# Half of an output projection inside the attention, operand pieces in a pool of nine, and four column blocks ahead of the last norm

## The chip, the cores and the metric

The kernel runs on one core of a Trainium2 chip. The metric is the device time of one execution in microseconds (us), the median of several runs. The core has five engines with queues of their own: TensorE (PE) for matrix products and transposes, VectorE (DVE), ScalarE (ACT), GpSimd (POOL), and SyncE (SP), which here issues nearly all DMA transfers. Each engine works through its own list in order; between engines the work is ordered by semaphores.

## The reference, cut

One layer of an encoder over two groups of tokens, a prompt of 512 and a sample of 1024, in float32. Attention and a state-space scan work side by side on each group; their outputs are gated, added and projected, then a norm, a residual sum and a SwiGLU feed-forward follow.

```python
proj = h @ w_in
att = rmsnorm(diff_attention(q, k, v, lam, rel_bias), subln_w) * (1.0 - lam_init)
y_ssm = rmsnorm((y_f + y_b + d_skip * xs) * silu(z), ssm_norm_w)
merged = g[:, :, 0] * (att @ w_proj_attn) + g[:, :, 1] * (y_ssm @ w_proj_ssm)
x = x + rmsnorm(merged @ w_out, norm_post_mix)
h = rmsnorm(x, norm_pre_ffn)
gate, up = split(h @ w_gate_up)
x = x + rmsnorm((silu(gate) * up) @ w_down, norm_post_ffn)
```

The model width is 1024 (8 blocks of 128), the feed-forward 2816 wide (22 blocks of 128).

## The kernel before

All products are made from split operands: a float32 value is a high part (`hi`) and the rest (`lo`), and each product of two 128-row blocks takes three matmuls (`gemm`, lines 167 to 169). `split` makes the two parts; "act_dve" casts on ACT (L135) and subtracts on DVE (L136), "act_pool" casts on ACT (L141) and subtracts on POOL (L142). `split_panel` does so for a 1024 x 256 weight panel. The code issues work in program order, and a scheduler that runs a timeline model while the kernel is built then settles each engine's order; pools of tiles with a fixed number of buffers set when a tile can be reused.

The stages: input projections; prompt attention and scans; then the three that matter here.

- `ph2`: the sample's attention, 8 heads of 8 query tiles of 128. A query tile needs scores on PE, a bias and minimum (L296) on DVE, an exponential (L299) on ACT, an addition of the two softmax maps (L304, `last_add`), transposes (L308), copies and lower parts (L311, L312), and the product with v into `o`. The attention gives way (`yield`) 64 times in all, and each time `run` adds `RATIO` to what is due of `side_work`, which has 32 units: the prompt's `w_proj_attn` (into `m_d`) and `w_proj_ssm` of three chunks of 512 tokens (`part_d`). After the last head, `mean_square` (L326, L327) sums squares of the output.
- `ph3`, first part. `load_merged(0)` reads the prompt's merged rows back and splits them (L891, L892). `att_scale(1)` makes the scales of the sample's heads (L334 to L344) and stores them in `r_d`. `aT1 = att(1)` loads, for each of eight heads, the attention rows and the scales (L349, L351), multiplies them (L352) and splits them, in a ring `araw` of three buffers. Then `out_proj(m0)`, `merge(1, aT1)`, `norms(0)`, `att(2)`, `out_proj(m1)`, `merge(2)`, `norms(1)`, `out_proj(m2)`, `norms(2)`. `out_proj` is 384 matmuls of 256 columns with copies and sums of squares on ACT (L1048, L1050); `norms` (L1057 to L1080) applies the post-norm, adds the input rows (L1065 to L1067), stores `x2_d`, applies the pre-norm (L1074), transposes on PE (L1078) and stores `h2_d`.
- The feed-forward. `Operands` reads `h2_d` for 768 tokens and makes seven operands `b11, t2, t3, t1, b21, t4, b22` (a seven-product scheme for two-by-two blocks); `t4` is three subtractions and additions on data of `b21` and `t2` (L951 to L953). `weights(jb)` makes the seven weight combinations of a column block, four of them on POOL (L989 to L997). `gate_up` does seven products of 12 matmuls with 384 columns, 84 a block. Blocks `jb < NPRE` come before `norms(2)`; after all 22, a second set of operands is made for the other 768 tokens, with `t4` and `b22` on POOL, and 22 more blocks follow. A last stage is the down projection.

The pool `big` holds seven tiles of 16 KB a partition: first the split pairs of `m` and `aT`, later one tile for each operand.

Of the kernel before, what the change touches and what calls it, by code (L numbers as in the profile page):

```python
# [18 lines left out]
P = 128  # L19
D = 1024  # L20
# [13 lines left out]
OT = ("gt", 2)  # L34
NG = 2
YE = ("act_pool",) * 4
RATIO = 0.5
QS = 0
IA = 1
AHEAD = (0,)  # L40
XRB = 2
NPRE = 2
CB = (1, 1)
RWB = 7
NW = 0
NKEEP = 1
SEQS = ((0, 4), (4, 12))
GROUPS = ((0, 512), (512, 1024))
# [29 lines left out]
def hybrid_trunk_kernel(ctx: ExitStack, tc: tile.TileContext, a: dict, y_prompt, y_sample):  # L78
# [5 lines left out]
    def f(ap):  # L84
        return ap.bitcast(F32)
# [26 lines left out]
    r_d = [dram.tile([32 * n, P], F32, name=f"r_d{n}") for n in (1, 2)]  # L112
    m_d = dram.tile([D, 512], F32, name="m_d")
    part_d = dram.tile([D, T], F32, name="part_d")
    x2_d = dram.tile([T, D], F32, name="x2_d")
    h2_d = dram.tile([D, T], F32, name="h2_d")
    ff_d = [dram.tile([DFF, 768], F32, name=f"ff_d{g}") for g in range(2)]
# [679 lines left out]

    ap = ctx.enter_context(tc.tile_pool(name="ap", bufs=1, reuse_waits="tile"))
    zq, msq = [ap.tile([P, 8, 8], F32, name=n) for n in ("zq", "msq")]
    with ExitStack() as ph2:  # L800
        qr = ph2.enter_context(tc.tile_pool(name="qr", bufs=2, reuse_waits="tile"))
        qk = ph2.enter_context(tc.tile_pool(name="qk", bufs=2, reuse_waits="tile"))
# [34 lines left out]
        def side_work():  # L837
            ahead = y_rows(0)
            aTt = yt.tile([P, 2, KB, 512], F32R, tag="yT", name="aTt", bufs=1)
            load_att(0, (aTt[:, 0], aTt[:, 1]), lambda: [t_[:, i] for t_ in [rp.tile([P, 2, 512], F32, tag="wraw", name="wraw")]  # L840
                                                 for i in range(2)])
            for r0 in range(0, D, P):
                gt = gated(r0, 0, slice(0, 512), panel(a["w_proj_attn"][0][:, r0:r0 + P]), (aTt[:, 0], aTt[:, 1]))
                store(out=m_d[r0:r0 + P, :], in_=gt)
                yield

            for c in range(NCH):
                cs = slice(c * 512, (c + 1) * 512)
                yTt = yt.tile([P, 2, KB, 512], F32R, tag="yT", name="yTt", bufs=1)
                for i_, raw in enumerate(ahead):  # L850
                    for j in (0, 2):
                        k = i_ * 4 + j
                        split(yTt[:, 0, k:k + 2], yTt[:, 1, k:k + 2], raw[:, j:j + 2], YE[k // 2])
                ahead = y_rows(c + 1)
                for r0 in range(0, D, P):
                    gt = gated(r0, D, cs, panel(a["w_proj_ssm"][0][:, r0:r0 + P]), (yTt[:, 0], yTt[:, 1]))
                    if c == 0:
                        mt = rp.tile([P, 512], F32, tag="wraw", name="mt")
                        load(out=mt, in_=m_d[r0:r0 + P, :])
                        G.tensor_add(gt, gt, mt)  # L860
                    store(out=part_d[r0:r0 + P, cs], in_=gt)
                    yield

        side = side_work()
        run(heads(512, 1024, range(8), pend, zq, msq, qk, pp, at, qr, s_ps, t_ps, o_ps),
            side, RATIO)
        for _ in side:
            pass
        pend.pop()()


    with ExitStack() as ph3:
        big = ph3.enter_context(tc.tile_pool(name="big", bufs=7, reuse_waits="tile"))
        wk = ph3.enter_context(tc.tile_pool(name="wk", bufs=2, reuse_waits="tile"))
        wy = ph3.enter_context(tc.tile_pool(name="wy", bufs=1, reuse_waits="tile"))
        mm = ph3.enter_context(tc.tile_pool(name="mm", bufs=6, space=PSUM, reuse_waits="tile"))
# [3 lines left out]
        def mm_tile(n):  # L880
            return mm.tile([P, n], F32, tag="mm", name="mm")

        def big_pair():
            return [big.tile([P, KB, 512], F32R, tag="big", name="big") for _ in range(2)]

        def load_merged(c):
            hi, lo = big_pair()
            for k in range(0, KB, 2):
                both = mp.tile([P, 2, 512], F32, tag="mt", name="both", bufs=4)
                load(out=both, in_=part_d[k * P:(k + 2) * P, c * 512:(c + 1) * 512].rearrange("(a p) t -> p a t", p=P))  # L890
                S.activation(out=hi[:, k:k + 2], in_=both, func=AF.Copy, scale=0.5)  # L891
                V.scalar_tensor_tensor(lo[:, k:k + 2], both, 0.5, f(hi[:, k:k + 2]), op0=ALU.mult, op1=ALU.subtract)  # L892
            return hi, lo

        def merge(c, aTt):
            cs = slice(c * 512, (c + 1) * 512)
# [20 lines left out]
        class Operands:  # L917
# [4 lines left out]
            def __init__(self, t0, pool, tag, bufs):  # L922
                self.t0, self.pool, self.tag, self.bufs, self.tiles = t0, pool, tag, bufs, {}
# [4 lines left out]
                load(out=x, in_=h2_d[r0:r0 + P, n0:n0 + 384])  # L928
                return x

            def build_first(self):
                b11, t2, t3, t1 = [big.tile([P, 2, 4, 384], F32R, tag="big", name="op") for _ in range(4)]
                self.tiles.update(b11=b11, t2=t2, t3=t3, t1=t1)
                for k in range(4):
                    x, y, z = self.raw(0, 0, k), self.raw(0, 1, k), self.raw(1, 1, k)
                    split(b11[:, 0, k], b11[:, 1, k], x[:], "act_dve")
                    V.tensor_sub(z, z, y)
                    split(t3[:, 0, k], t3[:, 1, k], z[:], "act_dve")
                    V.tensor_sub(y, y, x)
                    split(t1[:, 0, k], t1[:, 1, k], y[:], "act_dve")  # L940
                    V.tensor_add(x, x, z)
                    split(t2[:, 0, k], t2[:, 1, k], x[:], "act_dve")

            def build(self, names, add, eng):
                for name in names:
# [89 lines left out]
        with ExitStack() as ph3a:  # L1035
# [48 lines left out]
                return load_att(c, big_pair(), lambda: [  # L1084
                    wk.tile([P, 512], F32, tag="araw", name="araw", bufs=3) for _ in range(2)])

            m0 = load_merged(0)
            att_scale(1, zq, msq, ap, tr_ps, "tr")
            aT1 = att(1)
            t0 = out_proj(m0)  # L1090
            m1 = merge(1, aT1)
            norms(0, t0)
            aT2 = att(2)
# [2 lines left out]
            norms(1, t1)  # L1096
            ops = Operands(0, wk, "araw", 3)
            ops.build_first()
            ops.build(("b21",), V, "act_dve")
            t2 = out_proj(m2)  # L1100
            ops.build(("t4",), V, "act_dve")
            ops.tag, ops.bufs = OT
            ops.build(("b22",), V, "act_pool")
            w = {jb: weights(jb, "pt", 1) for jb in range(NPRE + NW)}
            for jb in range(NPRE):
                gate_up(0, jb, ops.all(), w[jb], mp, 1, False)
            norms(2, t2)

        with tc.tile_pool(name="fw", bufs=2, reuse_waits="tile") as fw:
            for jb in range(NPRE, FB):  # L1110
                if jb >= NPRE + NW:
                    w[jb] = weights(jb, rpool=fw if jb > NPRE else None)
# [99 lines left out]
```

## Time and profile before

| | |
|---|---|
| median of 3 runs | 3193.3 us (3192.85 to 3196.85) |
| the profiled execution | 3197.76 us |
| its span in the profile | 3196.0 us |
| mean granted clock of PE | 0.978 of full speed |
| PE busy over the span | 3044.8 us |
| DVE, ACT, POOL busy | 1837.5, 1256.7, 681.7 us |

A row of the profile names the line, the engine, the operation, and output and inputs by the program's names, with the time it was busy; "idle before" is the time in which that engine waited, and the arrow names the instruction that ended the wait. PEclk is the clock granted to PE, 1.00 being full speed.

### The profile page before, as it was taken

The page shows a single profiled execution, that of the slowest core. Times are in us where ns is not written, and L with a number is a line of the kernel's source. Part 1 is how long each engine was busy: PE and PEld are TensorE (multiplying, and loading weights), DVE is VectorE, ACT ScalarE, POOL GpSimd, SP SyncE. Part 2 cuts the span into 40 slices and gives each one's busy share as a digit, 9 for nine tenths or more (in the row PEclk, how much of TensorE's full clock was granted, in tenths as well). Part 3 has the DMA queues.
Part 4 walks back from the last instruction along what each step waited for, and adds up shares of the span by engine and source line. Part 5 has one row for each costly group of instructions (what it writes and reads, how often), then busy time and mean ns, then how long its engine had stood idle before and what let it go on. Part 6 is the DMA issues. An engine that isn't in the chain of part 4 may idle for free. (4 is left out here: it accounts for less than half of the span.)

```text
span 3196.0 us, 44151 instructions
## 1 busy us (share of the span) xinstructions
PE 3044.8 (95%) x16667; PEld 2677.0 (84%) x16667; DVE 1837.5 (57%) x2953; ACT 1256.7 (39%) x2301; POOL 681.7 (21%) x520
## 2 busy tenths in 40 slices
PE   8999999999999999899999898978999899989998
PEld 7988887888887777788888787878999899978787
DVE  5214444455327996387878955686667765632444
ACT  4103333333303333366666645543333333332343
POOL 0001111000133442243332100023333433210100
PEclk9999999999999999999999999989999999999999
DMA  4633333123554444755546047644333333363454
GB/s 149 195 99 113 112 104 106 57 79 106 152 170 136 147 143 149 212 173 167 165 137 186 27 139 239 218 141 136 103 98 105 97 103 91 114 203 97 124 163 132
DMA packets 443165, 430.35 MB, mean 135 GB/s; under 512 B 25232, under 2 KB 360305, under 8 KB 441841
## 3 DMA queue, kind: packets, MB, share of 16 engines
q1 hardware_dynamic: 442953, 427.55, 43.3%
q8 instruction: 131, 2.15, 0.3%
q14 instruction: 81, 0.66, 0.1%
HBM read 315.40 MB, written 120.44 MB: 136 GB/s over the span
## 5 line engine op out<-in xcount | busy, mean ns | idle before, releaser
L167 PE MATMUL acc<-hT,whi 128*128 128x512 f32 x1056 | 421.4, 399 | 4.0 <-ACT st L453 4.0
L168 PE MATMUL acc<-hT,whi 128*128 128x512 f32 x1056 | 416.7, 395 | 0.0
L169 PE MATMUL acc<-hT,wlo 128*128 128x512 f32 x672 | 262.2, 390 | 0.0
L167 PEld LDWEIGHTS acc<-hT,whi 128*128 128x128 f32 x1056 | 199.0, 188 | 50.2 <-issue 5.8
L299 ACT ACTIVATE pt<-pt,nm 128x1024 f32<-128x1024 f32 (+1 forms) x192 | 193.1, 1006 | 109.9 <-DVE nm L296 106.6
L168 PEld LDWEIGHTS acc<-hT,whi 128*128 128x128 f32 x1056 | 199.1, 189 | 42.7 <-issue 3.6
L296 DVE CUSTOM_DVE_ANT_0 pt<-s,tb 128x1024 f32<-128x1024 f32 (+1 forms) x192 | 197.5, 1041 | 52.4 <-PE s L294 40.4
L167 PE MATMUL acc<-whi,hT 128*128 128x256 f32 x768 | 225.2, 293 | 1.2 <-DVE st L374 0.6
L169 PE MATMUL acc<-whi,hT 128*128 128x256 f32 x768 | 225.6, 294 | 0.5 <-DVE hT L207 0.3
L168 PE MATMUL acc<-wlo,hT 128*128 128x256 f32 x768 | 224.2, 292 | 0.0
L169 PE MATMUL d<-dhi,fl 128*128 128x512 f32 x528 | 207.8, 393 | 8.9 <-DVE fl L136 8.9
L167 PE MATMUL d<-dhi,fh 128*128 128x512 f32 x528 | 207.7, 393 | 6.8 <-ACT fh L135 6.8
L168 PE MATMUL d<-dlo,fh 128*128 128x512 f32 x528 | 207.1, 392 | 0.0
L135 ACT CAST whi<-wraw 128x1024 fp32r<-128x1024 f32 (+1 forms) x115 | 115.9, 1036 | 213.8 <-PE acc L169 83.1
L136 DVE TENSOR_TENSOR fl<-raw,fh 128x896 fp32r<-128x896 f32 (+1 forms) x72 | 86.0, 1195 | 198.1 <-ACT fh L135 190.2
L234 POOL TENSOR_TENSOR ql<-raw,qh 128x512 fp32r<-128x512 f32 x48 | 65.3, 1373 | 577.3 <-ACT qh L231 567.9
L167 PE MATMUL mm<-op,wy 128*128 128x384 f32 x528 | 178.8, 339 | 9.5 <-ACT op L135 7.3
L169 PE MATMUL mm<-op,wy 128*128 128x384 f32 x528 | 178.6, 338 | 0.0
L168 PE MATMUL mm<-op,wy 128*128 128x384 f32 x528 | 178.3, 338 | 0.0
L136 DVE TENSOR_TENSOR wlo<-wraw,whi 128x1024 fp32r<-128x1024 f32 x80 | 97.1, 1243 | 114.9 <-ACT whi L135 105.6
L135 ACT CAST fh<-raw 128x896 fp32r<-128x896 f32 (+1 forms) x72 | 70.8, 983 | 225.8 <-PE d L168 189.9
L167 PEld LDWEIGHTS acc<-whi,hT 128*128 128x128 f32 x768 | 148.3, 193 | 12.1 <-issue 10.0
(358 smaller groups left out, 8325.0 us busy)
## 6 DMA issues: line engine op xcount, KB each, us to landing
wraw<-in_w_in_dram SPq DMA_DIRECT2D x60, 512.0 KB
wraw<-in_w_gate_up_dram SPq DMA_DIRECT2D x92, 256.0 KB
raw<-ff_d SPq DMA_DIRECT2D x48, 448.0 KB
wr<-in_w_gate_up_dram SPq DMA_DIRECT2D x80, 256.0 KB
ff_d<-c SPq DMA_DIRECT2D x88, 192.0 KB
g_d<-st SPq DMA_DIRECT2D x48, 256.0 KB
xg<-xs_d SPq DMA_DIRECT2D x48, 256.0 KB
gt<-g_d SPq DMA_DIRECT2D x48, 256.0 KB
```

The costliest lines, as they stand in the source:

```text
L135: S.copy(hi, raw)
L136: V.tensor_sub(lo, raw, f(hi))
L167: TE.matmul(ps, ah, bh, start=(i == 0), stop=False)
L168: TE.matmul(ps, ah, bl, start=False, stop=False)
L169: TE.matmul(ps, al, bh, start=False, stop=(i == n - 1))
L234: G.tensor_sub(q_l[:, s_], q_r[:, s_], f(q_h[:, s_]))
L296: V.tensor_tensor_reduce(out=pt[:], in0=sps[:], in1=tb[:, off:off + SL], scale=-1.0, scalar=3.0e38, op0=ALU.add, op1=ALU.min, accum_out=nm ...
L299: S.activation(out=pt, in_=pt, func=AF.Exp, bias=nm[:, m:m + 1], scale=-1.0, accum_out=(z0, zs[:, 0:1])[m])
```

## The change

It does four things.

1. The pool `big` becomes nine tiles of 12 KB. A pair of `m` or `aT` takes three tiles (class `Part` finds the part and block); an operand takes one.
2. `out_proj(m0)` goes from `ph3` into `side_work` as 16 units of 24 matmuls, with `RATIO` at 0.625, so 40 units are taken during the heads. The first eight use the buffer `f_ps`; the last eight (`LATE`) use score buffers `s_ps` and are tied behind the last addition by `issue_after`. Results go to `mo_d`, the sums of squares to `sums0`, and `ph3` loads them back as `t0`. `pend.pop` and `att_scale(1)` are issued ahead of the last eight units.
3. `t4` is issued together with `b21`, ahead of `out_proj(m2)`; the first weights are issued ahead of `b22`, whose splits now use DVE for the lower part. `NPRE` is 4, and weights are issued block by block.
4. In the second operand set `b11` and `t2` are issued first, with `t2`'s additions on POOL, then `t3` and `t1`, with DVE.

```diff
-RATIO = 0.5
+RATIO = 0.625
+LATE = 8
-NPRE = 2
+NPRE = 4
-NW = 0
...
+            m0 = yt.tile([P, 2, KB, 512], F32R, tag="yT", name="m0", bufs=1)
+            for k in range(0, KB, 2):
+                both = rp.tile([P, 2, 512], F32, tag="wraw", name="both")
+                load(out=both, in_=part_d[k * P:(k + 2) * P, 0:512].rearrange("(a p) t -> p a t", p=P))
+                S.activation(out=m0[:, 0, k:k + 2], in_=both, func=AF.Copy, scale=0.5)
+                V.scalar_tensor_tensor(m0[:, 1, k:k + 2], both, 0.5, f(m0[:, 0, k:k + 2]), op0=ALU.mult, op1=ALU.subtract)
+            for i in range(16):
+                p0, j = i // 4 * 256, i % 4
+                if j == 0:
+                    w = split_panel(a["w_out"][0][:, p0:p0 + 256])
+                if i < 16 - LATE:
+                    ps = f_ps.tile([P, 512], F32, tag="f", name="f")[:, 0:256]
+                else:
+                    ps = s_ps.tile([P, 1024], F32, tag="s", name="late")[:, 0:256]
+                with tc.issue_after(last_add[-1].ins) if i >= 16 - LATE else nullcontext():
+                    gemm_tm(ps, w, (m0[:, 0], m0[:, 1]), slice(j * P, (j + 1) * P))
+                mo = yt.tile([P, 512], F32, tag="gt", name="mo")
+                S.copy(mo[:, 0:256], ps)
+                S.activation(out=mo[:, 256:512], in_=ps, func=AF.Square, accum_out=sums0[:, j, i // 4:i // 4 + 1])
+                store(out=mo_d[j * P:(j + 1) * P, p0:p0 + 256], in_=mo[:, 0:256])
+                yield
...
+        pend.pop()()
+        att_scale(1, zq, msq, ap, t_ps, "t")
         for _ in side:
             pass
-        pend.pop()()
...
-        big = ph3.enter_context(tc.tile_pool(name="big", bufs=7, reuse_waits="tile"))
+        big = ph3.enter_context(tc.tile_pool(name="big", bufs=9, reuse_waits="tile"))
...
         def big_pair():
-            return [big.tile([P, KB, 512], F32R, tag="big", name="big") for _ in range(2)]
+            tiles = [big.tile([P, 2, 3, 512], F32R, tag="big", name="big") for _ in range(3)]
+            return Part(tiles, 0), Part(tiles, 1)
...
-            m0 = load_merged(0)
-            att_scale(1, zq, msq, ap, tr_ps, "tr")
             aT1 = att(1)
-            t0 = out_proj(m0)
+            t0 = [mp.tile([P, D], F32, tag="mt", name="mt", bufs=4) for _ in range(4)], sums0
+            for j, mt in enumerate(t0[0]):
+                load(out=mt, in_=mo_d[j * P:(j + 1) * P, :])
...
-            ops.build(("b21",), V, "act_dve")
+            ops.build(("b21", "t4"), V, "act_dve")
             t2 = out_proj(m2)
-            ops.build(("t4",), V, "act_dve")
             ops.tag, ops.bufs = OT
-            ops.build(("b22",), V, "act_pool")
-            w = {jb: weights(jb, "pt", 1) for jb in range(NPRE + NW)}
+            w = {0: weights(0, "pt", 1)}
+            ops.build(("b22",), V, "act_dve")
             for jb in range(NPRE):
+                if jb:
+                    w[jb] = weights(jb, "pt", 1)
                 gate_up(0, jb, ops.all(), w[jb], mp, 1, False)
...
             ops = Operands(768, fw, "rw", RWB)
-            ops.build_first()
+            ops.build(ops.names[:2], G, "act_dve")
+            ops.build(ops.names[2:4], V, "act_dve")
             ops.build(ops.names[4:], G, "act_dve")
```

How the orders move, at three places. First PE, behind the end of the sample's attention: `rt` is the transpose of the scales (L341 before, L342 now), `late` a late unit of the output projection, `ms` the sum of squares, `mm<-big,whi` of 512 columns `merge(1)`. Before, the scales' transpose stands among the matmuls of `out_proj(m0)`:

```order
L168 MATMUL mm<-wlo,big 128x256
L169 MATMUL mm<-whi,big 128x256
L341 MATMUL rt<-ident,att_r 64x128
L167 MATMUL mm<-whi,big 128x256
L168 MATMUL mm<-wlo,big 128x256
L169 MATMUL mm<-whi,big 128x256 x2
```

Now:

```order
L169 MATMUL late<-wlo,m_15511 128x256
L170 MATMUL late<-whi,m_15511 128x256
L327 MATMUL ms<-onec,av 128x1 x4
L342 MATMUL rt<-ident,att_r 64x128
L168 MATMUL mm<-big,whi 128x512 x4
L169 MATMUL mm<-big,whi 128x512
L170 MATMUL mm<-big,wlo 128x512
```

The output projection has moved ahead of the scales, and `merge(1)` follows them at once.

On SP, at the same place, the store of the scales `r_d` and the loads of `aT1`, one of scales and one of attention rows (`att_d`) for each head. Before, few other transfers stand between them:

```order
L344 DMA r_d_82<-rt 64x128
L351 DMA araw<-r_d_82 128x512
L349 DMA araw<-att_d 128x512
L351 DMA araw<-r_d_82 128x512
L349 DMA araw<-att_d 128x512
L351 DMA araw<-r_d_82 128x512
L154 DMA wraw<-in_w_out_dram 128x4x256 x2
L349 DMA araw<-att_d 128x512
```

Now (`xr` is an input row for the residual sum of `norms(0)`, `x_d` the store of its result):

```order
L345 DMA r_d_82<-rt 64x128
L352 DMA araw<-r_d_82 128x512
L350 DMA araw<-att_d 128x512
L1094 DMA x_d<-mt 128x1024
L1090 DMA xr<-in_x_prompt_dram 128x512 x2
L352 DMA araw<-r_d_82 128x512
L350 DMA araw<-att_d 128x512
L1090 DMA xr<-in_x_prompt_dram 128x512
L1094 DMA x_d<-mt 128x1024
L352 DMA araw<-r_d_82 128x512
```

Transfers of `norms(0)` have moved in between the loads of the heads.

Second, POOL at the start of the feed-forward: `op<-rw,op` are the lower parts of `b22`, `s` the weight combinations of a block. Before:

```order
L142 TENSOR_TENSOR op<-rw,op 128x384 x2
L989 TENSOR_TENSOR s_18811<-wraw 128x512
L990 TENSOR_TENSOR s_18812<-s_18811,wraw 128x512
L142 TENSOR_TENSOR op<-rw,op 128x384
L992 TENSOR_TENSOR s_18813<-wraw 128x512
L142 TENSOR_TENSOR op<-rw,op 128x384
```

Now:

```order
L146 TENSOR_TENSOR vl<-raw,vh 128x1024
L1014 TENSOR_TENSOR s_18818<-wraw 128x512
L1015 TENSOR_TENSOR s_18819<-s_18818,wraw 128x512
L1017 TENSOR_TENSOR s_18820<-wraw 128x512
L1022 TENSOR_TENSOR s_18819<-wraw,s_18819 128x512
```

The lower parts of `b22` have left POOL, and the first weights follow directly on the last work of the attention (`vl`).

Third, POOL at the sixth and seventh block of the first set, where the second operand set begins: `rw<-rw` are the differences and sums of `t2`. Now:

```order
L1015 TENSOR_TENSOR s_19703<-s_19702,wr 128x512
L983 TENSOR_TENSOR rw<-rw 128x384 x3
L1022 TENSOR_TENSOR s_19703<-wraw,s_19703 128x512
L1014 TENSOR_TENSOR s_19843<-wr,wraw 128x512
L1017 TENSOR_TENSOR s_19845<-wr 128x512
L983 TENSOR_TENSOR rw<-rw 128x384 x2
```

Before, only weight combinations stood there, and nothing of the second set was made on POOL but `t4`. The eight rows for `t2` are new.

More of the change, by code (lines that the diff above doesn't have):

```diff
@@ L114, in hybrid_trunk_kernel @@
     part_d = dram.tile([D, T], F32, name="part_d")
+    mo_d = dram.tile([512, D], F32, name="mo_d")
     x2_d = dram.tile([T, D], F32, name="x2_d")
@@ L799, in hybrid_trunk_kernel @@
     zq, msq = [ap.tile([P, 8, 8], F32, name=n) for n in ("zq", "msq")]
+    sums0 = ap.tile([P, 4, 4], F32, name="sums0")
     with ExitStack() as ph2:
@@ L881, in mm_tile, with __init__, __getitem__ @@
             return mm.tile([P, n], F32, tag="mm", name="mm")
-        def big_pair():
-            return [big.tile([P, KB, 512], F32R, tag="big", name="big") for _ in range(2)]
[L886 to L893, printed above, removed]
+        class Part:
+            def __init__(self, tiles, part):
+                self.tiles, self.part = tiles, part
+            def __getitem__(self, at_):
+                k = at_[1]
+                return self.tiles[k // 3][(at_[0], self.part, k % 3) + at_[2:]]
+        def big_pair():
+            tiles = [big.tile([P, 2, 3, 512], F32R, tag="big", name="big") for _ in range(3)]
+            return Part(tiles, 0), Part(tiles, 1)
         def merge(c, aTt):
@@ L929, in raw, with build_first @@
                 return x
-            def build_first(self):
-                b11, t2, t3, t1 = [big.tile([P, 2, 4, 384], F32R, tag="big", name="op") for _ in range(4)]
-                self.tiles.update(b11=b11, t2=t2, t3=t3, t1=t1)
+            def build_first(self, names=("b11", "t2", "t3", "t1")):
+                o = {n: big.tile([P, 2, 4, 384], F32R, tag="big", name="op") for n in names}
+                self.tiles.update(o)
                 for k in range(4):
                     x, y, z = self.raw(0, 0, k), self.raw(0, 1, k), self.raw(1, 1, k)
[L936 to L942, printed above, removed]
+                    for n, t_, m, s_ in (("b11", x, None, None), ("t3", z, z, y), ("t1", y, y, x), ("t2", x, x, z)):
+                        if m is not None and (n in o or n != "t1"):
+                            (V.tensor_add if n == "t2" else V.tensor_sub)(t_, m, s_)
+                        if n in o:
+                            split(o[n][:, 0, k], o[n][:, 1, k], t_[:], "act_dve")
             def build(self, names, add, eng):
@@ L1110, in hybrid_trunk_kernel @@
             for jb in range(NPRE, FB):
-                if jb >= NPRE + NW:
-                    w[jb] = weights(jb, rpool=fw if jb > NPRE else None)
+                w[jb] = weights(jb, rpool=fw if jb > NPRE else None)
                 gate_up(0, jb, ops.all(), w[jb], fw, 2)
             ops = Operands(768, fw, "rw", RWB)
-            ops.build_first()
+            ops.build(ops.names[:2], G, "act_dve")
+            ops.build(ops.names[2:4], V, "act_dve")
             ops.build(ops.names[4:], G, "act_dve")
```

## The prediction

> **What bounds the kernel now.** I read the page first, for the engine that carries the span and where it is not full; then windows, which say how full each engine is in the stretches that the change touches; then waits and the timeline at their edges.
>
> ```profile
> span 3196.0 us, 44151 instructions
> PE 3044.8 (95%) x16667; PEld 2677.0 (84%) x16667; DVE 1837.5 (57%) x2953; ACT 1256.7 (39%) x2301; POOL 681.7 (21%) x520
> PE   8999999999999999899999898978999899989998
> ```
>
> TensorE (PE) is the bound, 95% busy, and the change removes no matmul (the order of both has the same number). So time can only come out of PE's stalls. A slice is 79.9 us; the weakest that the change touches is the 27th (digit 7, 2077 to 2157). Finer:
>
> ```profile
> core 0: us, PE busy (x) PEld busy (x) DVE busy (x) ACT busy (x) POOL busy (x), PEclk, DMA share, GB/s
> ...
> 1780.00:1800.00 20.00, 18.76 (x124) 16.09 (x122) 19.79 (x38) 15.36 (x28) 0.00 (x0) 1.00 0.04 14
> 1831.00:1848.00 17.00, 11.58 (x76) 10.86 (x75) 4.46 (x8) 5.35 (x9) 0.00 (x0) 0.80 0.15 47
> 1848.00:1896.00 48.00, 48.00 (x388) 48.00 (x389) 23.01 (x40) 20.26 (x52) 0.00 (x0) 0.97 0.42 133
> ...
> 1960.00:1980.00 20.00, 14.49 (x98) 13.65 (x99) 6.21 (x8) 12.54 (x30) 0.00 (x0) 0.86 0.64 210
> 2006.00:2050.00 44.00, 44.00 (x198) 36.51 (x197) 34.08 (x68) 21.36 (x39) 0.00 (x0) 1.00 0.73 239
> 2100.00:2120.00 20.00, 4.53 (x26) 3.70 (x25) 16.68 (x32) 9.46 (x23) 9.58 (x6) 0.68 0.27 80
> 2160.00:2180.00 20.00, 12.13 (x48) 9.40 (x49) 7.64 (x22) 7.50 (x12) 2.54 (x2) 0.66 0.52 175
> ...
> 2480.00:2500.00 20.00, 12.57 (x62) 11.80 (x62) 19.84 (x23) 8.56 (x17) 15.92 (x13) 0.83 0.25 75
> 2500.00:2520.00 20.00, 20.00 (x117) 20.00 (x116) 14.15 (x22) 6.67 (x13) 7.88 (x6) 1.00 0.39 119
> ```
>
> Columns after the length are busy time per engine, then the granted clock. Attention (1780 to 1800) is bound by VectorE (DVE), 19.79 of 20. Behind the last tile PE loses 5.4 us of 17 (1831 to 1848); then `out_proj(m0)` fills 48 us without a gap. Three weak stretches follow: 1960, 2100 to 2180, 2480.
>
> **Part A: the prompt's output projection goes into the attention.** The edges before:
>
> ```profile
> 1830.93 1.19 DVE L304 SCALAR_TENSOR_TENSOR pt<-pt,zs 128x1024 f32<-128x1024 f32 x1
> ...
> 1848.36 0.16 DVE L327 COPY msq<-ms 128x4 f32<-128x4 f32 x1 [8.60 <-PE ms L326]
> ...
> 1856.14 0.23 DVE L339 TENSOR_TENSOR att_r<-att_r,att_t 128x64 f32<-128x64 f32 x1
> ...
> 1863.21 0.75 DVE L352 SCALAR_TENSOR_TENSOR araw<-araw,cols 128x512 f32<-128x512 f32 x1 [5.91 <-DMA araw<-r_d]
> ...
> 1895.38 0.75 DVE L352 SCALAR_TENSOR_TENSOR araw<-araw,cols 128x512 f32<-128x512 f32 x1 [1.81 <-DMA araw<-r_d]
> ```
>
> ```profile
> L352 DVE SCALAR_TENSOR_TENSOR araw<-araw,cols 128x512 f32<-128x512 f32 x9 | 6.8, 752 | 20.4 <-DMA araw<-r_d 20.4
> L136 DVE TENSOR_TENSOR wlo<-wraw,whi 128x1024 fp32r<-128x1024 f32 x6 | 7.1, 1219 | 0.0
> L892 DVE SCALAR_TENSOR_TENSOR big<-both,big 128x1024 fp32r<-128x1024 f32 x4 | 4.9, 1222 | 0.0
> ...
> 1728.00:1831.00 103.00, 90.59 (x561) 0.97 0.28 87
> ...
> 2006.46 0.40 PE L167 MATMUL mm<-big,whi 128*128 128x512 f32 x1
> ```
>
> The chain from the last addition (L304) through the scales (L339) to the eighth head of `aT1` (L352) lasts 64 us, and the 48 us of `out_proj(m0)` lie over it. That is the cover the change takes away: PE's next row behind the late units is `merge(1)`, whose first products go head by head. Step by step:
> - Last addition: DVE, already full, gets 4 lower halves of `m0` (1.222) and 4 of the two early weight panels (1.219): 9.8 us, so 1840.7. PE gets the 192 matmuls of the early units at 48.00/388 = 0.124, 23.8 us; its free 12.4 of 1728 to 1831 (90.59 of 103, where the two orders part) and the 9.8 hold 22.2, so PE nearly binds too, and 1.6 is an error of this step. ScalarE (ACT) gets about 14 us of casts, copies and squares and has 4.6 free in each 20; the 16 stores of the results and their 4 loads go where DMA is at 0.04.
> - Mean squares: the edge puts the late units behind the last addition, and the mean squares and scales stand behind them on PE: 23.8 us, and an estimated 4.5 for the last transposes and `o` (under half of the 11.58 of 1831 to 1848, the rest standing between the late units): 1869.
> - Scales: 1848.36 to 1856.14 was 7.8, with 4 lower halves of 1.22 in it. The new order has 2 of those and 4 rows of `norms(0)` there, 10 us by the same rows: 1879. To the first head as before, 7.1: 1886.
> - Eight heads, spaced (1895.38 − 1863.21)/7 = 4.60: last one 1918; its split about 2, its 12 matmuls at 44.00/198 = 0.222, 2.7: 1923.
> - What is left to `merge(2)`: 96 matmuls at 0.222 (21.3), 384 at 0.124 (47.6), 20 transposes (about 4), and 3 for the wait on `norms(0)` that 1960 to 1980 shows at 5.5: 1999.
>
> Before, `merge(2)` began at 2006.5. **Gain 7.** The unknown is the spacing, now with the loads and stores of `norms(0)` between the pairs of loads. The quickest pair before is 3.98 apart (1863.21 to 1867.19), the slowest 6.13; 4.60 is nearest since the same 20.4 us of DMA wait carry it. Ends: +12 and −4.
>
> **Part B: start of the feed-forward, four column blocks ahead of the last norm.**
>
> ```profile
> 2118.89 0.69 PE L167 MATMUL mm<-op,whi 128*128 128x384 f32 x1 [15.37 <-ACT whi L135]
> ...
> 2164.69 2.58 PE L1078 MATMUL tr_ps<-ident,mt 128*128 128x128 f32 x8 [7.67 <-DVE mt L1074]
> 2167.84 5.41 PE L1078 MATMUL tr_ps<-ident,mt 128*128 128x128 f32 x24 [0.56 <-ACT hr L1080]
> 2175.83 0.69 PE L167 MATMUL mm<-op,whi 128*128 128x384 f32 x1 [2.58 <-ACT whi L135]
> ...
> 2110.34 4.14 POOL L142 TENSOR_TENSOR op<-rw,op 128x384 fp32r<-128x384 f32 x2 [299.38 <-DVE rw L951]
> 2114.44 1.66 POOL L989 TENSOR_TENSOR s<-wraw 128x512 f32<-128x512 f32 x1
> 2116.17 2.01 POOL L990 TENSOR_TENSOR s<-s,wraw 128x512 f32<-128x512 f32 x1
> ...
> 2113.07 0.55 DVE L953 TENSOR_TENSOR rw<-rw,op 128x384 f32<-128x384 f32 x1
> ...
> L136 DVE TENSOR_TENSOR op<-rw,op 128x384 fp32r<-128x384 f32 x5 | 2.8, 557 | 1.4 <-ACT op L135 1.4
> L184 DVE TENSOR_TENSOR mt__19093<-mr 128x4 f32<-128x4 f32 x3 | 3.1, 1042 | 0.0
> ...
> 2107.20:2160.60 53.40, 49.82 (x83) 0.81 0.41 128
> ```
>
> PE waits 15.37 us for a weight made from L990 on GpSimd (POOL), which stands behind two splits of `b22`. These go to DVE. But the `s` of L989 takes a buffer of the same ring of three as `t4`'s subtractions, which still come before it and whose third ends at 2113.6 (L953). So some 1.6 us of the 15.37 go and 13.8 stay. The wait of 7.67 goes: PE has two more blocks of 84 matmuls to do while DVE does `norms(2)`.
>
> But DVE, busy 49.82 of 53.40 there (last row), gets those blocks too. A block takes PE 84 × 20/117 = 14.4 us at the rate of 2500 to 2520, and DVE 14.15/20 of that, 10.2. So DVE has 49.8, two blocks 20.4, the four splits of `b22` 2.2 (0.557 each), L1074 about 2.7 and the second root's nine small rows, at 1.04 and less, about 6: 81 us from 2107, and the fourth block ends at 2188. The transposes follow at their 8.6 (2164.69 to 2173.25, paced by ScalarE's copies): 2196.6. In both orders 12 matmuls of the next block stand ahead of them, in the new one beside DVE's last additions. Before, four blocks and transposes were done at 2173.25 + 2.58 + 28.8 = 2204.6. **Gain 8.** Ends 2 (DVE's rows slow down as those near 2480 do, 0.81 for 0.55) and 14 (DVE keeps under PE).
>
> **Part C: second operand set.**
>
> ```profile
> 2490.00 1.10 PE L167 MATMUL mm<-op,wy 128*128 128x384 f32 x2 [7.34 <-ACT op L135]
> ...
> L136 DVE TENSOR_TENSOR op<-rw,op 128x384 fp32r<-128x384 f32 x28 | 21.7, 813 | 0.2 <-ACT op L135 0.2
> L951 POOL TENSOR_TENSOR rw<-op 128x384 f32<-128x384 f32 x4 | 7.1, 1788 | 10.8 <-DVE op L136 10.8
> L952 POOL TENSOR_TENSOR rw<-rw,op 128x384 f32<-128x384 f32 x4 | 5.3, 1332 | 0.0
> L953 POOL TENSOR_TENSOR rw<-rw,op 128x384 f32<-128x384 f32 x4 | 5.0, 1270 | 0.0
> ```
>
> Around 2480 PE waits 7.34 us for `t4` of the second set, made on POOL in 17.4 us that begin after 10.8 of waiting for a split on DVE, itself full (19.84 of 20). With nine pieces two operands (`b11`, `t2`) are made earlier, between blocks 4 and 6, with `t2`'s 8 operations on POOL. That takes 8 splits at 0.813 and 4 additions, about 9 us, off DVE here, so POOL starts up to 9 us sooner and the 7.34 go. The stall as a whole is about 12: the 7.34, at most 20 × 0.17 = 3.4 that the clock of 0.83 costs, and 1 to 2 of short waits ahead; some 4 stay. **Gain 8**, ends 3 and 11. At blocks 4 to 6 POOL gets 8 operations of about 1.4, 11 us, beside the 7.88 of 20 it uses there; DVE is at 14.15 of 20. I charge 0 to 3 us, **1** in the sum.
>
> A rule against this: the Trainium skill, "SBUF — State Buffer", section "Who interferes with whom", says that a VectorE instruction with two SBUF inputs and a GpSimd instruction that reads SBUF exclude each other for the whole instruction. The 0.813 of the split while POOL is busy 15.92 of 20 agrees; by that rule `t2`'s 11 us of POOL would delay DVE by as much over two blocks, and its 10 us of slack there would take it, so 0 to 1 us by the rule.
>
> **Sum:** 7 + 8 + 8 − 1 = 22. The profiled execution is 3197.8 (3196.0 and 1.8 around the span), 4.5 above the median 3193.3; so 3176 for such an execution, **3171** against the median.
>
> **Rivals.**
> - *The tail gives nothing (3178).* PE's 14 us wait ahead of the first head and the spacing eat part A, B and C stay (15). For it: the cover of 48 us is gone. A special form is the clock: 1831 to 1848 has 0.80 and 2160 to 2180 0.66 at 61% busy, and `merge(1)` would be 2.7 busy in 4.6, 59%. At half clock a head's matmuls take 5.4 > 4.6: 8 × 0.8 = 6.4 us more. Against: single waits there are 1.9 us, and attention at 18.76 of 20 keeps 1.00. The Trainium skill, "TensorE: Matmul & The Clock Gate", section "HAM oscillation — how this bites in real kernels", puts the danger at idle gaps above about 3.4 us; by that the clock would hold here. Chance 0.17.
> - *More than I count (3156).* Heads at 3.98, DVE under PE in the four blocks, all of 2480's stall: 12 + 14 + 11 = 37. Against: DVE's 49.82 of 53.40. Chance 0.13.
> - *The change doesn't do what it says at 2100 (3177).* First weights no sooner, and the 7.67 only becomes a wait of blocks 2 to 4 on DVE: B gives 2. For it: the ring of three. Chance 0.09.
> - *Slower (3210).* SP serves its queue in order; in the new order four stores of `norms(0)`'s rows and seven of its loads stand between the pairs of `aT1`'s loads. If a store waits for a row that DVE does between heads, that head's loads wait too: each costs up to one landing, 5.9 us (L352's first wait). Four such waits cost 23.6 and decide: no gain; seven, 41: 17 slower. For it: nothing covers the chain any more. Against: the order puts the first four rows of `norms(0)` ahead of the chain, and DMA is at 0.42 there. Chance of no gain 0.09, of slower 0.08.
>
> The forecast itself has 0.44. Under about 0.2% (6.4 us) a measurement of this kernel can't tell a change from none. Faster by more: 0.44 + 0.17 + 0.13 + 0.09 less 0.03 for tails = **0.80**; within: **0.12**; slower: **0.08**. Leaving out the slower cases and the ends of the others, the range is **3151 to 3190**; its top is about the sum of the low ends (−4 + 2 + 3), its bottom that of the high ones, 37, and 5 for what the steps leave out.
>
> **What would show it.** After: the last addition (L304) at 1840, the first head near 1886 and heads 4.6 apart, `merge(2)` before 2000; from 2100 one PE wait of 13 to 14 us and no wait of PE on L1074's rows ahead of the transposes; DVE over 95% busy in the four blocks; PE's wait for `t4` near 2480 below 4 us. Wrong if the heads are 8 us apart, if attention lengthens by over 15 us (PE and DVE then bind in turn), or if DVE's rows near blocks 4 to 6 stretch PE's blocks beyond 14.4.

## The result and the profile after

The changed kernel takes **3215.8 us** (median of 6, 3214.4 to 3218.1) against 3193.1 us before (median of 6, 3188.0 to 3196.9): ratio 1.0066, 95% interval 1.0055 to 1.0077. It is slower by about 21 us, where 22 us faster was forecast. The profiled execution took 3215.7 us, so its trace stands for the median. Executions of one kernel differ by up to 20 us, and one of the run with the late units behind the scales took 5023 us and is in no ratio below.

The page of the changed kernel, with the span, PE's busy time and its 40 slices of 80.3 us:

```profile
span 3213.9 us, 44231 instructions
...
PE 3034.4 (94%) x16667; PEld 2667.4 (83%) x16667; DVE 1853.3 (58%) x2957; ACT 1255.8 (39%) x2301; POOL 683.9 (21%) x524
...
PE   7999999999999999899998968978999999989998
```

PE does the same matmuls in 10 us less of busy time but in a span 18 us longer: the loss is waiting. The new digit 6 is the 24th slice, 1848 to 1928, right behind the attention. In windows (busy time and count of PE, PEld, DVE, ACT and POOL, granted clock, DMA share, GB/s):

```profile
1728.00:1760.00 32.00, 24.61 (x165) 20.96 (x164) 29.24 (x45) 25.24 (x39) 8.92 (x6) 1.00 0.65 201
1760.00:1800.00 40.00, 39.27 (x295) 37.13 (x293) 33.14 (x59) 28.79 (x58) 6.99 (x4) 1.00 0.30 95
1800.00:1846.00 46.00, 43.86 (x301) 38.62 (x300) 42.62 (x78) 33.33 (x62) 3.45 (x2) 1.00 0.12 41
...
1875.00:1896.00 21.00, 0.40 (x1) 0.13 (x1) 13.56 (x43) 4.64 (x11) 0.00 (x0) 0.58 0.78 263
1896.00:1933.00 37.00, 29.47 (x108) 21.76 (x108) 19.61 (x39) 10.66 (x23) 0.00 (x0) 0.87 0.63 203
```

The same stretches of the kernel before:

```profile
1728.00:1760.00 32.00, 28.95 (x173) 24.69 (x172) 28.40 (x47) 21.92 (x36) 6.01 (x5) 0.95 0.66 212
1760.00:1800.00 40.00, 34.53 (x217) 29.66 (x215) 37.43 (x67) 28.66 (x52) 8.06 (x6) 0.96 0.14 40
```

Two things are to be seen. In the attention, from 1760 to 1800, PE goes from 34.53 to 39.27 of 40 while DVE falls from 37.43 to 33.14: in this stretch the bound has passed from DVE to PE. And from 1875 to 1896 PE is empty, with one matmul in 21 us; the clock falls to 0.58 there.

The ends of the steps of part A, on DVE (last addition, last sums of squares, last row of the scales, first and eighth head) and on PE (transpose of the scales, `merge(1)`, `merge(2)`):

```profile
1845.79 1.19 DVE L305 SCALAR_TENSOR_TENSOR pt<-pt,zs 128x1024 f32<-128x1024 f32 x1
...
1874.97 0.16 DVE L328 COPY msq<-ms 128x4 f32<-128x4 f32 x1 [10.91 <-PE ms L327]
...
1885.43 0.22 DVE L340 TENSOR_TENSOR att_r<-att_r,att_t 128x64 f32<-128x64 f32 x1
...
1894.97 0.75 DVE L353 SCALAR_TENSOR_TENSOR araw<-araw,cols 128x512 f32<-128x512 f32 x1 [3.60 <-DMA araw<-r_d]
...
1928.55 0.75 DVE L353 SCALAR_TENSOR_TENSOR araw<-araw,cols 128x512 f32<-128x512 f32 x1 [1.48 <-DMA araw<-r_d]
```

```profile
1885.79 0.40 PE L342 MATMUL rt<-ident,att_r 128*64 128x128 f32 x1 [10.86 <-DVE att_r L340]
1896.48 2.07 PE L168 MATMUL mm<-big,whi 128*128 128x512 f32 x4 [10.30 <-ACT big L136]
...
2016.47 0.39 PE L168 MATMUL mm<-big,whi 128*128 128x512 f32 x1
```

From the last addition to `merge(2)` it was 175.5 us before (1830.93 to 2006.46) and is 170.7 now, though 24 us of PE's work have left that stretch.

Further on, the first matmuls of the 44 column blocks, read from both traces, show a second loss. Block 6 takes 20.0 us instead of 14.68, and blocks 9, 12, 15 and 18 take 15.8 to 16.0. Block 22, which holds the change of operand sets, takes 27.8 where it took 26.8. On SP and PE at block 6:

```profile
2239.79 9.37 SPq L955 DMA_DIRECT2D rw<-h_d  x8
2249.25 0.93 SPq L999 DMA_DIRECT2D wr<-in_w_gate_up_dram  x2
```

```profile
2249.43 0.41 PE L168 MATMUL mm<-op,wy 128*128 128x384 f32 x1 [2.50 <-ACT c L1046]
...
2292.02 0.45 PE L168 MATMUL mm<-op,wlo 128*128 128x384 f32 x1 [0.86 <-DVE c L1051]
```

SP spends 9.4 us on eight loads for the second operand set, and the weights' load stands behind them. From then on the weights of each block come late: POOL, at block 9, waits 9.6 us for them, where it waits 7.9 us at the same block in the kernel before.

```profile
2285.87 1.29 POOL L1014 TENSOR_TENSOR s<-wr,wraw 128x512 f32<-128x512 f32 x1 [9.60 <-DMA wraw<-in_w_gate_up_dram]
```

### The profile page after: what moved, and what is told of

It is laid out like the page before. It is cut to its first block, busy times and chain, and to the rows that moved or that the text cites. A ratio compares the mean times of both kernels' runs of the same rounds, so it can differ in the third digit from the quotient of the medians.

```text
span 3213.9 us, 44231 instructions
## 1 busy us (share of the span) xinstructions
PE 3034.4 (94%) x16667; PEld 2667.4 (83%) x16667; DVE 1853.3 (58%) x2957; ACT 1255.8 (39%) x2301; POOL 683.9 (21%) x524
## 4 chain that ended last, share of the span: by engine, by line
PE 67%; DMA 11%; DVE 10%; issue 5%; ACT 3%; POOL 2%; SPq 1%; ACTq 0%; DVEq 0%; POOLq 0%
PE acc L168 9%; PE acc L170 9%; PE acc L169 9%; PE mm L170 4%; PE mm L168 4%; PE mm L169 4%; PE d L170 4%; PE d L169 4%; PE d L168 4%; DMA wraw<-in_w_gate_up_dram 1%; PE s L294 1%; PE t L309 1%; PE s L295 1%; DMA araw<-r_d 1%; PE f L169 1%
## 5 line engine op out<-in xcount | busy, mean ns | idle before, releaser
L168 PE MATMUL acc<-hT,whi 128*128 128x512 f32 x1056 | 421.5, 399 | 3.6 <-ACT st L454 3.6
L169 PE MATMUL acc<-hT,whi 128*128 128x512 f32 x1056 | 416.9, 395 | 0.0
L169 PE MATMUL mm<-op,wy 128*128 128x384 f32 x528 | 181.3, 343 | 2.7 <-DVE op L137 2.6
L168 PE MATMUL mm<-op,wy 128*128 128x384 f32 x528 | 181.0, 343 | 2.5 <-ACT c L1046 2.5
L170 PE MATMUL mm<-op,wy 128*128 128x384 f32 x528 | 180.8, 342 | 0.2 <-DVE wy L137 0.2
L170 PE MATMUL acc<-hT,whi 128*128 128x512 f32 x384 | 156.3, 407 | 0.0
```

Of the source, the lines that this page charges most:

```text
L168: TE.matmul(ps, ah, bh, start=(i == 0), stop=False)
L169: TE.matmul(ps, ah, bl, start=False, stop=False)
L170: TE.matmul(ps, al, bh, start=False, stop=(i == n - 1))
```

## The experiments

All times are medians, each with its ratio to the kernel before in runs on the same chip. Traces are compared from the last addition on, and times by their ratios. Code is shown in part (`...`).

**Each part undone, and the pool alone.** The second operand set as before:

```diff
-            ops.build(ops.names[:2], G, "act_dve")
-            ops.build(ops.names[2:4], V, "act_dve")
+            ops.build_first()
```

> The changed kernel with the second operand set made as before, all of it behind block 21 of the first set. Theory: the early part of that set (t2's eight operations on POOL, the splits and loads beside the blocks) costs the 5.3 us of block 6 and the 1.2 us of every third block after it; blocks 5 to 21 all go back to 14.65 us, and the time falls by 11 to 13 us, to about 3204. Rival: the every-third wait comes from the four blocks ahead of the norm and the weights issued one by one; then only block 6 recovers and the time is about 3210.

The output projection back behind the attention:

```diff
-RATIO = 0.625
+RATIO = 0.5
...
+            m0 = load_merged(0)
+            att_scale(1, zq, msq, ap, tr_ps, "tr")
             aT1 = att(1)
-            t0 = [mp.tile([P, D], F32, tag="mt", name="mt", bufs=4) for _ in range(4)], sums0
...
+            t0 = out_proj(m0)
```

> The changed kernel with the prompt's output projection back behind the attention, as before (its merged rows split per block of 128). Theory: the projection in the attention and the uncovered chain to aT1 cost 10 us by the start of merge(2), of which 6.5 are left at the first feed-forward product; the time falls by 6 to 10 us, to 3206 to 3210. Rival: the cost is made up elsewhere and the time stays within 2 us of 3215.8.

The start of the feed-forward as before:

```diff
-NPRE = 4
+NPRE = 2
...
-            ops.build(("b21", "t4"), V, "act_dve")
+            ops.build(("b21",), V, "act_dve")
             t2 = out_proj(m2)
+            ops.build(("t4",), V, "act_dve")
...
-            ops.build(("b22",), V, "act_dve")
+            ops.build(("b22",), V, "act_pool")
+            w = {jb: weights(jb, "pt", 1) for jb in range(NPRE)}
```

> The changed kernel with the start of the feed-forward as before: two blocks ahead of the norm, t4 behind the last projection, b22 split on POOL, weights ahead of the blocks. Theory: the four blocks gain 5.7 us (offset 6.5 at the first product, 0.7 behind the transposes), so without them the time is about 3221. Rival: the every-third wait of blocks 9 to 18 goes with them; then about 3215.

The kernel before with the pool of nine alone (with it, the prompt's merged rows are split per block of 128 rows and not two blocks at a time):

```diff
-            return [big.tile([P, KB, 512], F32R, tag="big", name="big") for _ in range(2)]
+            tiles = [big.tile([P, 2, 3, 512], F32R, tag="big", name="big") for _ in range(3)]
+            return Part(tiles, 0), Part(tiles, 1)
```

> The kernel before with the pool of nine 12 KB pieces alone (the prompt's merged rows are split per block of 128 instead of two blocks). Theory: the pieces lie elsewhere in memory, so the first down-projection weights wait for the last products, as seen in the changed kernel (4 us between the last block and the end): about 3197. Rival: placement is harmless and that delay comes from another part: 3193 within 2.

| kernel | us | ratio to before | 95% interval |
|---|---|---|---|
| as changed | 3215.8 | 1.0066 | 1.0055 to 1.0077 |
| second set as before | 3205.6 | 1.0038 | 1.0018 to 1.0058 |
| projection as before | 3192.7 | 1.0005 | 0.9993 to 1.0016 |
| start as before | 3223.2 | 1.0099 | 1.0084 to 1.0114 |
| pool of nine alone | 3186.5 | 0.9979 | 0.9969 to 0.9988 |

The second set costs about 10 us (11 to 13 were expected), and blocks 9 to 18 are back at 14.65 us; but block 6 still takes 20.7 there, against the expectation, so that one isn't owed to the new order of the set. The projection aside costs 20 us (0.0061 between the two ratios), twice what was expected from the trace. The start gains 7 to 11 us. The pool alone gains 6.7 us, against both expectations. The delay at the down projection isn't the pool's: from the first matmul of the last block to the end the pool alone takes 407.2 us, the kernel before 406.6, the changed kernel 410.7.

**The late units behind the scales.** The tie of the eight late units is moved from the last addition to the transpose of the scales:

```diff
-        att_scale(1, zq, msq, ap, t_ps, "t")
+        last_add.append(att_scale(1, zq, msq, ap, t_ps, "t"))
```

(`att_scale` returns its transpose.)

> The changed kernel with the eight late units tied behind the transpose of the scales instead of behind the last addition. Theory (the late units hold up the chain that starts behind the attention, and leave it uncovered afterwards): mean squares and scales come 12 to 15 us earlier, the late units fill PE's empty 21 us, merge(2) begins 12 to 17 us earlier, and the time is about 3201. Rival (the heads of aT1 are paced by the transfers of norms(0) between them): the heads end as late as now and the time is within 4 us of 3215.8.

3208.1 us (1.0033, 1.0021 to 1.0046), which is 10.5 us of the 20 by the ratios, and 7 us above the theory's 3201. On DVE and PE:

```profile
1842.44 1.19 DVE L305 SCALAR_TENSOR_TENSOR pt<-pt,zs 128x1024 f32<-128x1024 f32 x1
```

```profile
1861.38 0.39 PE L342 MATMUL rt<-ident,att_r 128*64 128x128 f32 x1 [4.15 <-DVE att_r L340]
...
1874.34 0.39 PE L168 MATMUL late<-whi,m 128*128 128x256 f32 x1 [1.18 <-ACT mo L886]
...
2001.84 0.39 PE L168 MATMUL mm<-big,whi 128*128 128x512 f32 x1
```

The scales come 18.9 us behind the last addition instead of 40.0, and `merge(2)` 159.4 behind it instead of 170.7: the 11.3 us of the trace fit the 10.5 of the times. So the late units, standing ahead of the sums and scales on PE, held the chain up, and were then missing as its cover. The rival gives little: with none of the transfers of `norms(0)` between their loads, as here, the heads are 4.38 us apart instead of 4.80, 3 us in all.

**Pool and start together; both tail and second set mended; t2 on DVE.** The first leaves the projection and second set as before; the second is the last run with `ops.build_first()`; the third:

```diff
-            ops.build(ops.names[:2], G, "act_dve")
+            ops.build(ops.names[:2], V, "act_dve")
```

> The kernel before with the pool of nine and the new start of the feed-forward (t4 early, weights block by block, four blocks ahead of the norm), but the output projection and the second operand set as before. Theory: the parts add, 6 us by the pool and 7 to 10 by the start: 3177 to 3180. Rival: the gain of the start is against a start that the pool of nine had spoilt (block 4 took 18.5 us there), so together they give little more than the pool alone: 3184 to 3188.

> As the run with the late units behind the transpose of the scales, and the second operand set made as before. Theory: both gains add, 14 and 10 us: about 3191. Rival: the second set's cost hangs on the phase in which the weights run behind the blocks, and shifts with the tail: 3197 or more.

> The changed kernel with t2 of the second set added on DVE instead of POOL, the early order kept. Theory: POOL's eight operations hold up the weights that POOL makes, so block 6 and every third block recover and the time falls by 6 to 10 us, to 3206 to 3210. Rival: the early loads and splits in the in-order queues of ACT and DVE do it, whichever engine adds: 3214 to 3218.

Pool and start: 3185.6 us, 0.9962 (0.9947 to 0.9977), the fastest of all and faster than both kernels. The value lies in the rival's range; the intervals of this and of the pool alone (0.9969 to 0.9988) overlap, so that the start adds to the pool is not shown by this pair. Late units behind the scales with the old second set: 3193.8 us, 1.0002 (0.9989 to 1.0015): the two gains add, 11.5 and 9.9 us by the ratios. t2 on DVE: 3205.4 us, 1.0034 (1.0021 to 1.0047), as fast as with the whole set made as before. The cost of the new order of the second set thus goes with t2's additions on POOL. In that trace block 9 takes 14.65 us again, and the weights' loads are issued 5.4 us behind the start of block 9 instead of 9.5. Block 6 still takes 21.2:

```profile
2254.57 0.69 PE L168 MATMUL mm<-op,wlo 128*128 128x384 f32 x1 [3.84 <-DVE c L1052]
```

**All sixteen units behind the scales**, `RATIO` 0.5 and `LATE` 16, with the old second set.

> As the run with the late units behind the scales and the second operand set as before, but with no unit of the output projection in the attention: all sixteen stand behind the transpose of the scales (48 us of PE), 0.5 units a step. Theory: the eight early units lengthen an attention in which PE has become the bound, and nothing behind it gets shorter for them, since the chain to aT1 sets the time there; without them the last addition comes 12 to 18 us earlier and the time falls from 3193.8 to 3182 to 3186. Rival: they cost nothing net (what the attention loses is saved behind it), and the time stays at 3192 to 3196.

3203.7 us, 1.0048 (1.0033 to 1.0063): 10 us by the medians and 15 by the ratios slower than with eight of them in the attention (1.0002), and both expectations are missed. The last addition came at 1827.9, 14.5 us sooner than with eight early units. But the sixteen units take the stretch from 1847 to 1903:

```profile
L168 PE MATMUL late<-whi,m 128*128 128x256 f32 x128 | 37.9, 296 | 5.9 <-ACT mo L886 5.9
```

384 matmuls that took 48 us as `out_proj` take 56, partly since PE waits 5.9 us for ACT's copies of results, and all of them stand behind the scales, where the old `out_proj` begins 9 us ahead of the scales and runs around them. So the theory that the early units are a plain loss falls: they lengthen the attention by about 14 us and save more than that behind it, where what follows is covered (`merge(1)` at 1896.6 in the run with eight late units behind the scales, at 1903.7 here).

**Half aside, the other half as before.** Eight units in the attention; the other half of the projection in the next stage, untied:

```diff
-            t0 = out_proj(m0)
+            t0 = out_proj(m0, sums0, 512)
```

> Pool of nine and new start, second set as before, and half of the prompt's output projection aside as in the change; its other half is done in the stage behind the attention as before (after its merged rows are read and split again), where the sums of squares and the scales can stand among its matmuls. Theory: the early half lengthens the attention by about 14 us, and of the 24 us that it takes off the stretch behind, most is lost to the chain from the last addition to aT1 (64 us before), so there is no gain: 3183 to 3190 against 3185.6. Rival: with the scales among the late half the chain is covered, and the full difference of 10 us comes out: 3174 to 3178.

3190.3 us, 0.9991 (0.9980 to 1.0003), against 0.9962 without anything aside: no gain, but some 5 us lost (9 by the ratios).

```profile
1842.90 1.19 DVE L305 SCALAR_TENSOR_TENSOR pt<-pt,zs 128x1024 f32<-128x1024 f32 x1
```

```profile
1901.91 1.53 PE L168 MATMUL mm<-big,whi 128*128 128x512 f32 x4 [3.05 <-ACT big L136]
...
2001.82 0.39 PE L168 MATMUL mm<-big,whi 128*128 128x512 f32 x1
```

`merge(1)` begins at 1881.8, 23.5 us sooner after the last addition than with the whole projection behind it (38.9 against 62.4 in the pool-and-start run). Yet `merge(2)` begins only 8.9 sooner after it (158.9 against 167.8), since PE now waits for heads. The 14 us by which the attention is longer are not earned back: 8.9 of 24 us come out. This is the theory's case, at the upper end of its range.

**The second set held back.** Pool and start, with the first four operands of the second set tied behind the last addition of block 14, and of block 21:

```diff
+            with tc.issue_after(hold[HOLD].ins):
+                ops.build_first()
```

> The kernel with the pool of nine and the new start (run before: 3185.6), with the first four operands of the second set tied behind the last addition of block 14. Theory: with nine pieces the scheduler begins the second set at blocks 4 to 6, where the weights have no lead yet, and the 6 us that these blocks lose go: 3178 to 3181, blocks 4 to 6 at 14.65 except for the norm. Rival: the blocks lose that time to the weights' late start behind the norm, whatever the second set does: 3184 to 3188.

> As the run in which the first four operands of the second set were tied behind block 14, now behind the last addition of block 21, so that none of them is made beside the blocks. Theory: early operands cost some 4 us at whichever block they stand (block 16 took 19.05 us in that run), so without any the blocks 4 to 6 and 16 are clean and the time falls below the 3185.6 of pool and start alone: 3179 to 3183. Rival: what is saved in the blocks is paid at the boundary (over 31 us for block 22 instead of 27): 3185 to 3190.

3193.5 us, 0.9998 (0.9983 to 1.0014), and 3191.5 us, 0.9989 (0.9979 to 1.0000): both are slower than pool and start (0.9962), so both theories are missed, and only the rival of the second comes near, with its long block 22. The lengths of some blocks, from the starts of their first matmuls (block 4 holds the norm's transposes in kernels with the new start):

| kernel | 5 | 6 | 9 | 16 | 22 |
|---|---|---|---|---|---|
| before | 14.68 | 14.68 | 14.68 | 14.68 | 26.82 |
| as changed | 14.85 | 20.00 | 15.79 | 14.65 | 27.79 |
| second set as before | 14.85 | 20.72 | 14.65 | 14.65 | 25.33 |
| t2 on DVE | 14.65 | 21.23 | 14.65 | 14.65 | 24.89 |
| pool and start | 15.91 | 17.43 | 14.65 | 14.65 | 27.69 |
| held to block 14 | 14.65 | 15.25 | 15.79 | 19.05 | 27.19 |
| held to block 21 | 14.65 | 14.65 | 14.65 | 14.65 | 31.91 |

With the set held, blocks 5 and 6 lose little or nothing; with it made early, they lose 4 to 7 us in this table even where the code has `build_first` behind block 21. SP's loads for the second set show why: in blocks 4 to 6 there are none in the kernel before, 10 with pool and start, and 28 in the changed kernel. In the run with the pool alone it is block 4, which holds no norm there: 18.5 for 14.68. So nine pieces alone let the scheduler begin the set at once, and the cost follows the set: block 16 when held to 14, the boundary when held to 21 (31.91, and 16.52 for block 23), where PE waits for ACT's casts, as these rows of the last run show:

```profile
2460.90 0.69 PE L169 MATMUL mm<-op,whi 128*128 128x384 f32 x1 [2.74 <-ACT op L137]
...
2479.15 1.10 PE L169 MATMUL mm<-op,wy 128*128 128x384 f32 x2 [1.80 <-ACT op L137]
```

Held to block 14, the kernel takes 4.3 us longer than pool and start from block 5 to block 23, held to block 21 2.1 us; the rest of the difference lies ahead of block 5 and is not explained.

The table shows one thing more. Held to block 14, nothing of the second set is made in blocks 5 to 14, and t2 is on DVE; yet block 9 takes 15.79 us, as in the changed kernel. What the five traces with such waits (the changed kernel, projection as before, start as before, late units behind the scales, held to block 14) have in common is a lag: the load of the second half of a block's weights (`wraw`) is issued 8.2 to 10.2 us behind the start of block 7, in the nine other traces 5.1 to 7.8. So t2's additions on POOL are one way into that lag, and not the only one.

## Why the prediction was wrong

The forecast was 22 us faster, from 7 + 8 + 8 − 1. By differences of ratios the runs give +20 to +24 for the projection aside (part A), −5 to −11 for the start (B), +9 to +14 for the second set (C), and −6.7 for the pool, which had no term: in all about +19, where +21 was measured.

- **Part A, "Gain 7": wrong in sign, and the largest error.** The step that failed is the tail. From the last addition to `merge(2)` the sum allowed 158 us (1840.7 to 1999), 17 less than the 175.5 of before; the trace shows 170.7, as much as the pool of nine has with the *whole* projection still in that stretch (170.8, between these rows):

```profile
1830.32 1.18 DVE L305 SCALAR_TENSOR_TENSOR pt<-pt,zs 128x1024 f32<-128x1024 f32 x1
```

```profile
2001.09 0.39 PE L168 MATMUL mm<-big,whi 128*128 128x512 f32 x1
```

  So the 24 us of PE's work that left the stretch bought nothing there. The text had the mechanism ("That is the cover the change takes away") and counted the chain without its cover, but its lengths were too short: the first head comes 49.2 us behind the last addition for 45.3, and the heads are 4.80 apart for 4.60. From the end of the last head's products to `merge(2)` it takes 83.4 us (1933.1 to 2016.5) for 76: "3 for the wait on `norms(0)`" became 9.4 us of waits, 2.0 for a weight (first row) and 7.4 for ACT (the two others, of 1959 to 1990; total, times, longest):

```profile
1936.19 0.56 PE L170 MATMUL mm<-big,wlo 128*128 128x512 f32 x1 [1.97 <-DVE wlo L137]
...
PE mm L168 <- ACT msq L1075: 4.9, 1, 4.9
PE mm L168 <- ACT big L939: 2.5, 1, 2.5
```

  The second term that failed is the attention: forecast 9.8 us longer, it is 14.9 longer (last addition at 1845.79 for 1830.93). In the seven traces with early units the last addition comes at 1842 to 1854, in the seven without at 1822 to 1831. PE's free time, on which the sum drew, was in part not used: 7.4 us are left free in 1728 to 1760 (24.61 busy of 32). So the tail gains 4.8 us against the kernel before, which the pool of nine alone gains too (4.7), and the attention loses 14.9. With the 4 us at the end that come with the late units (below) that is 19 of the 20 to 24. And the place of the late units, which the text described ("mean squares and scales stand behind them on PE"), costs 11 us as the run with the other tie shows; it was counted as a matter of course, not as a choice with a price.
- **Part C, "Gain 8": wrong in sign.** The step that failed is that the stall at the boundary ends with the wait for `t4`: that wait of 7.34 did go, but waits of PE on DVE took its place, and block 22 takes 27.8 us where 26.8 less 8 was forecast:

```profile
2493.84 0.66 PE L168 MATMUL mm<-op,wlo 128*128 128x384 f32 x1 [3.27 <-DVE c L1052]
...
2505.43 0.44 PE L169 MATMUL mm<-op,wy 128*128 128x384 f32 x1 [2.60 <-DVE op L137]
```

  The other step that failed is the price "0 to 3 us, 1 in the sum" beside blocks 4 to 6, which was counted from busy shares (POOL 7.88, DVE 14.15 of 20). From block 5 to block 23 the changed kernel takes 6.6 us longer than with the second set as before, 302.05 for 295.41. Of that, 5.0 us are in blocks 9, 12, 15 and 18, with the lag of the weights, and 2.5 in block 22; block 6 is as long in both (20.0 and 20.7), so it isn't the price of the new order. With t2 on DVE the lag goes and so does the cost. The queues are the likely link: SP's eight loads hold up the weights' loads by 9.4 us. That t2's additions slow the release of the load buffers, and so SP, is argued from the rows, not tried alone.
- **Part B, "Gain 8": right in size.** 7.4 us by medians, 10.5 by ratios, in the changed kernel; on top of the pool alone it gives 5.4 by the ratios, which is not clear of noise. The wait before the second weight stayed and did not shrink (16.46 us, in the row below, for a forecast of 13 to 14 and 15.37 before), and the 7.67 us ahead of the transposes went. DVE is not over 95% busy in the four blocks but 72.37 of 80 us (2120 to 2200), so it binds less than was thought.

```profile
2126.46 0.69 PE L168 MATMUL mm<-op,whi 128*128 128x384 f32 x1 [16.46 <-ACT whi L136]
```

- **The pool of nine** stood in the sum at nothing and gains 6.7 us. Its traces have 168 to 173 us from the last addition to `merge(2)` in five kernels with the old tail, against 175.5. Why was not tested; the finer split of the prompt's merged rows, which comes with the pool, is as open a candidate as the earlier operands.
- **The rivals.** "The tail gives nothing" was right about the tail, but it left out what the attention loses and kept B and C at 15. "Slower (3210)" came near the time by luck, for its mechanism isn't there: heads are 4.80 us apart and wait at most 3.6 for a transfer. (By its own terms, 41 against a gain of 22, it gives 19 slower, not 17.)
- **Left out:** 4 us between the last block and the end in the changed kernel. All runs with late units have 3 to 5 us more there than the kernel before, the others under 1. DVE's six lower parts of down-projection weights take 12.53 us for 8.59 before, and POOL makes two more beside them (first the changed kernel, then the kernel before):

```profile
2818.46 12.53 DVE L137 TENSOR_TENSOR dlo<-draw,dhi 128x1024 fp32r<-128x1024 f32 x6
...
2819.05 6.62 POOL L146 TENSOR_TENSOR dlo<-draw,dhi 128x1024 fp32r<-128x1024 f32 x2
```

```profile
2805.70 8.59 DVE L136 TENSOR_TENSOR dlo<-draw,dhi 128x1024 fp32r<-128x1024 f32 x6
...
2802.51 5.03 POOL L145 TENSOR_TENSOR dlo<-draw,dhi 128x1024 fp32r<-128x1024 f32 x2
```

  A row of DVE that stands alone takes 1.21 us. In the changed kernel two rows, from 2820.1 to 2826.7, lie beside POOL's and take 3.38 each; before, one does and takes 2.91. The six together are 3.9 us longer, about what is missing. Why the rows fall together in the runs with late units stays open, as does the period of three of the waits in blocks 9 to 18 (the weight sums use two buffers of a ring of three in each block; that this is the reason wasn't tried).

## What to carry to other kernels

Work that lies under a latency chain (steps that each wait for the one before) is its cover: before moving it away, count the chain alone from end to end, with the waits behind it; only what the work exceeds the chain by can be gained. With half of the projection aside that was 9 of 24 us, against 14 lost where the work went. Work that is put beside a steady loop can cost more than the busy share of its engine says, here about 10 us for 1; look first at what stands behind it in the queues, SP's loads above all. A part of a change that seems to be only preparation (here the pool's pieces) deserves a run of its own, since it was the part that gained.

## What the hardware showed

While PE waited 21 us with one matmul, the granted clock fell (0.58 in 1875 to 1896), and its mean was still 0.87 in 1896 to 1933, where the longest wait between two heads is 2.8 us. The half clock (0.50) lasts from 1878.5 to 1902.4, and comes again from 1909.2 to 1912.6. The Trainium skill, "TensorE: Matmul & The Clock Gate", section "Part 1: The HAM clock gate", has the array at half clock after an idle window of about 3.4 us; the trace agrees at the long gap, where half clock begins 3.6 us behind the last matmul. It does not agree at 1909.2, where the clock falls behind a wait of only 2.8 us.

The products of the first head and part of the third therefore ran at half speed, which the sum of the prediction had as full; it had held that gap of 3.4 us against waits of 1.9 us, and not against the 14 us ahead of the first head that it names itself. The loss is small here, since PE waits for heads again from 1916 on (1.41 and 1.35 us).
